# Two of four weight sums of each Strassen pair made by an accumulating DMA, with the weights stored as contiguous pairs of blocks

## Chip, cores and metric

One core of a Trainium2 chip runs the kernel. The metric is the device time of one execution in microseconds (us). TensorE is PE in the profile, VectorE is DVE, ScalarE is ACT, GpSimd is POOL and SyncE is SP.

## What is computed

A decoder block in float32 on 512 tokens of width 1024: two mixers side by side (retention with 4 heads, sliding-window attention with 8 query and 2 key heads), gated, merged and projected, then an MLP with squared ReLU of inner width 4096. Cut to what matters:

```python
h = rmsnorm(x, pre_mix_norm)
proj = h @ w_in                       # 1024 x 5888
q_r, k_r, v_r, g_r, q_s, k_s, v_s, gate_r, gate_s = split(proj)
y_r = (silu(g_r) * groupnorm(retention(q_r, k_r, v_r))) @ w_ret_out
y_s = sliding_window_attention(q_s, k_s, v_s, sinks) @ w_swa_out
merged = sigmoid(gate_r) * y_r + sigmoid(gate_s) * y_s
x = x + rmsnorm(merged @ w_out, post_mix_norm)
h = rmsnorm(x, pre_mlp_norm)
u = square(relu(h @ w_up))            # 1024 x 4096
x = x + rmsnorm(u @ w_down, post_mlp_norm)
```

The two gates are the last 2048 columns of `w_in`.

## The kernel before

Every product is made from split operands: `split` writes a float32 value as `hi + lo` (ACT casts `hi`, L106; DVE subtracts to get `lo`, L107), and `mm3` (L149 to L151) adds hi x hi, hi x lo and lo x hi in PSUM. A weight is loaded into a `raw` tile by SP (two buffers for the whole kernel) and split into `whi` and `wlo` (four buffers each).

The stages follow one another on PE: pre-norm and the first projections, four heads of retention and window attention, the window attention's output projection (`ys`), the gates with the retention's output projection (`yr`) between them, the output projection (`ps`), and the MLP.

For the gates and for 13 of the 16 pairs of `w_up` blocks, a pair of output blocks (256 columns) is made by one level of Strassen-Winograd: 7 block products instead of 8, each of 4 x 3 matmuls with 256 tokens. With the pair's weight cut into four quarters (`a11`, `a21` the first half of the contraction, `a12`, `a22` the second; the first index is the block of columns), `wino_weights` makes four sums:

- `s1 = a21 + a22` (L182) and `s3 = a11 + a21` (L183), the two halves of the tile `s31`, split into `p31`
- `s2 = s1 + a11` (L186) and `s4 = s2 + a12` (L187), the two halves of `s24`, split into `p24`

Besides, `p1` (`a11`, `a12`) and `p22` (`a22`) are splits of the quarters themselves. `p31` and `p1` lie in the `whi`/`wlo` buffers; `s31`, `s24`, `p24` and `p22` have one buffer each. `wino_pair` makes the products 11, s2, s1, s3, 12, s4 and 22 and combines them (DVE L218 to L229, ACT L217). `wino_tokens` makes the sums of the tokens once for the gates (`hsum`) and once for the MLP (`h2s`). Before the gates the tokens are put together as float32 in four places (`fb`): half of a `raw` buffer each for two, and the tiles `s31` and `s24` for the other two.

In the MLP the first three pairs of `w_up` blocks are plain products (`first_ups`, `up_half`, from `load_feature_pair`, L122), since half of the tokens come later. Then a quarter of a down projection (`load_moving`, L136, 48 matmuls of 512 columns) and an `up_pair` alternate; the last group has down projections alone.

The order on each engine is made by a scheduler when the kernel is built: by the order of the program, priorities (`tc.high_priority`) and its own estimate of when operands are ready. On the chip each engine keeps that order, and waits where an operand isn't there.

Of the kernel before, what the change touches and what calls it, by code (L numbers as in the profile page):

```python
# [20 lines left out]
KD = D_MODEL // P  # L21
# [7 lines left out]
EPS = 1e-6  # L29
# [8 lines left out]
C_QR, C_KR, C_VR, C_GR, C_QS, C_KS, C_GATE_R, C_GATE_S = (  # L38
    0, 512, 1024, 2048, 3072, 3584, 3840, 4864,
)  # L40
# [6 lines left out]
def decay_table():  # L47
    """[j, h, i]: gamma_h ** -(j + 1) / sqrt(dk) where i >= j, else 0; within a chunk."""
    pos = np.arange(P)
    t = np.where(  # L50
        pos[None, :] >= pos[:, None],
        np.exp(-log_gammas()[:, None, None] * (pos[:, None] + 1)), 0.0,
    )
    return np.ascontiguousarray((t * RET_DK**-0.5).transpose(1, 0, 2).astype(np.float32))


def chunk_table():
    """[j, 0, h]: gamma_h ** (127 - j) / sqrt(dk); [i, 1, h]: EPS * gamma_h ** (-2 (i + 1))."""
    pos, lg = np.arange(P)[:, None], log_gammas()[None, :]
    t = np.stack([np.exp(lg * (P - 1 - pos)) * RET_DK**-0.5, EPS * np.exp(-2 * lg * (pos + 1))], 1)  # L60
    return np.ascontiguousarray(t.astype(np.float32))


def distance_table():
    """[i, j]: distance of query i to key j of the two blocks, or MASKED / slope-free mask."""
    dist = (np.arange(P)[:, None] + P) - np.arange(2 * P)[None, :]
    return np.where((dist >= 0) & (dist < P), -dist, MASKED).astype(np.float32)

# [6 lines left out]
def block_kernel(ctx, tc, x, pre_mix, w_in, w_ret, w_swa, w_out, sinks, post_mix,  # L75
# [3 lines left out]
    w_in, w_ret, w_swa, w_out, w_up, w_down = (  # L79
        w[0] for w in (w_in, w_ret, w_swa, w_out, w_up, w_down)  # L80
    )
# [14 lines left out]
    def rstd_of(sumsq, n, scale):  # L96
        """(sumsq * scale + eps) ** -0.5, [P, n]."""
        ms = small.tile([P, 4], F32, name="ms")
        r = small.tile([P, 4], F32, name="rstd")
        nc.vector.tensor_scalar(ms[:, :n], sumsq, scale, EPS, op0=ALU.mult, op1=ALU.add)  # L100
        nc.gpsimd.tensor_tensor(r[:, :n], ms[:, :n], mhalf[:, :n], op=ALU.pow)
        return r

    def split(hi, lo, src):
        """src = hi + lo exactly, each with a significand that one pass carries."""
        nc.scalar.copy(hi, src)  # L106
        nc.vector.tensor_tensor(lo, src, f(hi), op=ALU.subtract)  # L107
# [10 lines left out]
    def load_feature_pair(w, c0):  # L118
        """Columns c0..c0+256 of w as two stationary blocks [k, kk, 128]."""
        nk = w.shape[0] // P  # L120
        raw = raw_tile([P, nk, 256])
        nc.sync.dma_start(raw, w[:, c0 : c0 + 256].rearrange("(k p) c -> p k c", p=P))  # L122
        return [parts(raw[:, :, b * P : (b + 1) * P], [P, nk, P]) for b in range(2)]

    def load_feature_blocks(w, cols):
        """Columns c..c+128 of w, for each c, as stationary blocks [k, kk, 128]."""
# [6 lines left out]
    def load_moving(w, r0, nr, c0, width):  # L133
        """Rows r0.. of w, columns c0..c0+width, as moving blocks, two tiles."""
# [24 lines left out]
    def wino_tokens(wx, b11, b12, b21, b22, f, dst):  # L159
        """b: (hi, lo) quadrants; f: their float32 copies, overwritten; dst: (hi, lo) of sums."""  # L160
# [13 lines left out]
    def wino_weights(wx, w, c0):  # L174
        """Columns c0..c0+256 of w: the seven left operands, (hi, lo) of [k, 4, 128]."""
        raw = raw_tile([P, KD, 256])
        nc.sync.dma_start(raw, w[:, c0 : c0 + 256].rearrange("(k p) c -> p k c", p=P))
        a11, a12 = raw[:, :4, :P], raw[:, 4:, :P]
        a21, a22 = raw[:, :4, P:], raw[:, 4:, P:]
        s31 = wx.tile([P, 2, 4, P], F32, name="s31")  # L180
        s24 = wx.tile([P, 2, 4, P], F32, name="s24")
        nc.vector.tensor_tensor(s31[:, 1], a21, a22, op=ALU.add)  # L182
        nc.vector.tensor_tensor(s31[:, 0], a11, a21, op=ALU.add)  # L183
        p31 = parts(s31, [P, 2, 4, P])
        p1 = parts(raw[:, :, :P], [P, KD, P])
        nc.vector.tensor_tensor(s24[:, 0], s31[:, 1], a11, op=ALU.add)  # L186
# [6 lines left out]
            "11": tuple(a[:, :4] for a in p1), "12": tuple(a[:, 4:] for a in p1),  # L193
            "22": tuple(p22),
            "s1": tuple(a[:, 1] for a in p31), "s3": tuple(a[:, 0] for a in p31),
# [3 lines left out]
    def wino_pair(wx, a, b, out):  # L199
        """out [P, 4, 256]: the two halves of block one, then those of block two, negated."""  # L200
# [30 lines left out]
    # ---- pools by phase  # L231
# [4 lines left out]
    def transpose_in(dst, src_of, half):  # L236
        """token-major [P, 1024] blocks (of two token blocks) -> feature-major hi, lo."""
# [13 lines left out]
    # ---- pre-norm of x, kv and first v projection by token block  # L251
# [22 lines left out]
    def norm_tokens(t):  # L274
        """Token block t of the normed input, transposed, as hi and lo."""
# [109 lines left out]
    def swa_scores(b, qs2):  # L385
        bias = dpool.tile([P, 2, 2 * P], F32, name="bias", bufs=2)
# [86 lines left out]
    # ---- retention, one head, by chunks of 128 tokens; token i of a chunk is carried  # L473
    # divided by gamma ** (i + 1), which the group norm takes out again
    def ret_keys(kT, h):
        """Token-major keys of the first three chunks, decayed to the chunk's end."""
# [24 lines left out]
    def ret_states(kd, v, h):  # L501
        """State before chunks 1, 2 and 3."""
# [114 lines left out]
    # ---- swa output projection  # L617
# [30 lines left out]
    # ---- gates  # L648
# [9 lines left out]
    fb = [fs[:, 0], fs[:, 1], wx.tile([P, 4, 256], F32, name="s31"), wx.tile([P, 4, 256], F32, name="s24")]  # L658
# [6 lines left out]
    def gate(name, bp):  # L665
        c0 = C_GATE_S if name == "s" else C_GATE_R
        a = wino_weights(wx, w_in, c0 + bp * 256)
# [14 lines left out]
    def ret_proj(bp):  # L682
        """Output projection of the retention, gated, plus the gated swa's, in sig."""
# [20 lines left out]
    # ---- output projections of both mixers, merge  # L704
# [33 lines left out]
    # ---- output projection, residual, pre-norm of the MLP  # L738
# [51 lines left out]
    # ---- MLP  # L790
# [19 lines left out]
    def up_half(fb, w, half):  # L810
        ps = bank([P, 256], "up")
        for k in range(KD):
            mm3(
                ps, (w[0][:, k, :], w[1][:, k, :]),
                tuple(a[:, k % 4] for a in quads[k // 4][half]), k == 0, k == KD - 1,
            )
        c = slice(half * 256, half * 256 + 256)
        rl = ppool.tile([P, 256], F32, name="rl")
# [20 lines left out]

    def first_ups(half, fps):  # L840
        for fp in fps:
            if half == 0 or fp == 0 and NH > 4:
                held[fp] = load_feature_pair(w_up, fp * 256)
# [23 lines left out]
    def up_pair(fp):  # L867
        a = wino_weights(wx, w_up, fp * 256)
# [16 lines left out]
    def finish(t, n):  # L885
        """Post-norm and residual of token block t, once acc's column half n is whole."""
# [72 lines left out]
_INS = ['x', 'pre_mix_norm', 'w_in', 'w_ret_out', 'w_swa_out', 'w_out', 'sinks', 'post_mix_norm',  # L959
# [20 lines left out]
```

## Time and profile before

| | |
|---|---|
| median of three runs | 774.61 us (774.47 to 774.65) |
| span of the profiled execution, first to last instruction | 772.8 us |
| the profiled execution's own time | no figure beside its span; the runs' median is 1.8 us above the span |
| PE busy | 761.1 us (98%), 4772 matmuls |
| DVE / ACT / POOL busy | 510.3 / 367.6 / 19.2 us |
| DMA | 78.21 MB, 101 GB/s in the mean |
| mean granted clock of TensorE | 0.997 |

Stages by the first matmul of each: gates from 254.0 us, output projection from 378.4, first up pairs from 423.7, Strassen up pairs and down projections from 460.2. A row of the timeline gives start and duration in us, engine (SPq is SP's queue of DMA issues), line, operation, output and inputs, shape, and in brackets how long the engine had been idle and what released it. A row of the waits gives who waited for what, then us in total, times, and the longest.

### The profile page before, as it was taken

The page shows a single profiled execution, that of the slowest core. Times are in us where ns is not written, and L with a number is a line of the kernel's source. Part 1 is how long each engine was busy: PE and PEld are TensorE (multiplying, and loading weights), DVE is VectorE, ACT ScalarE, POOL GpSimd, SP SyncE. Part 2 cuts the span into 40 slices and gives each one's busy share as a digit, 9 for nine tenths or more (in the row PEclk, how much of TensorE's full clock was granted, in tenths as well). Part 3 has the DMA queues.
Part 4 walks back from the last instruction along what each step waited for, and adds up shares of the span by engine and source line. Part 5 has one row for each costly group of instructions (what it writes and reads, how often), then busy time and mean ns, then how long its engine had stood idle before and what let it go on. Part 6 is the DMA issues. An engine that isn't in the chain of part 4 may idle for free.

```text
span 772.8 us, 11585 instructions
## 1 busy us (share of the span) xinstructions
PE 761.1 (98%) x4772; PEld 686.5 (89%) x4772; DVE 510.3 (66%) x841; ACT 367.6 (48%) x619; POOL 19.2 (2%) x30
## 2 busy tenths in 40 slices
PE   8999999999999999999999999999999999999996
PEld 6989889898888999999888999999999999999885
DVE  5474474655878888775954887665667675766364
ACT  6364454364644535333634785545544444444321
POOL 1100000000001000000011000000000000000000
PEclk9999999999999999999999999999999999999998
DMA  9151222312012333243571133333323333222402
GB/s 295 28 163 53 90 58 75 109 29 81 28 58 80 120 125 115 68 146 109 185 251 54 56 109 109 110 109 110 93 81 100 109 110 109 87 81 106 137 1 109
DMA packets 68038, 78.21 MB, mean 101 GB/s; under 512 B 1809, under 2 KB 55185, under 8 KB 67986
## 3 DMA queue, kind: packets, MB, share of 16 engines
q1 hardware_dynamic: 67986, 77.48, 31.3%
q8 instruction: 37, 0.61, 0.3%
q14 instruction: 15, 0.12, 0.1%
HBM read 75.38 MB, written 2.10 MB: 100 GB/s over the span
## 4 chain that ended last, share of the span: by engine, by line
PE 93%; DVE 3%; ACT 1%; issue 1%; DMA 1%; POOL 0%; SPq 0%; DVEq 0%; POOLq 0%; ACTq 0%
PE wino L149 9%; PE wino L151 9%; PE wino L150 9%; PE down L149 7%; PE down L150 7%; PE down L151 7%; PE pblk L151 5%; PE pblk L150 5%; PE pblk L149 5%; PE ptok L151 2%; PE ptok L150 2%; PE ptok L149 2%; PE yr L149 2%; PE ps L149 2%; PE ps L151 2%; PE yr L151 2%
## 5 line engine op out<-in xcount | busy, mean ns | idle before, releaser
L106 ACT CAST whi<-raw 128x1024 fp32r<-128x1024 f32 x103 | 107.9, 1051 | 127.1 <-PE down L151 57.7
L107 DVE TENSOR_TENSOR wlo<-raw,whi 128x1024 fp32r<-128x1024 f32 x103 | 125.4, 1221 | 63.0 <-ACT whi L106 53.6
L149 PE MATMUL down<-whi,u 128*128 128x512 f32 x256 | 99.8, 390 | 0.0
L150 PE MATMUL down<-wlo,u 128*128 128x512 f32 x256 | 99.7, 390 | 0.0
L151 PE MATMUL down<-whi,u 128*128 128x512 f32 x256 | 99.6, 389 | 0.0
L151 PE MATMUL pblk<-hT,wlo 128*128 128x512 f32 x160 | 62.4, 390 | 0.5 <-DVE wlo L107 0.5
L149 PE MATMUL pblk<-hT,whi 128*128 128x512 f32 x160 | 62.6, 391 | 0.0
L150 PE MATMUL pblk<-hT,whi 128*128 128x512 f32 x160 | 62.3, 390 | 0.0
L151 PEld LDWEIGHTS down<-whi,u 128*128 128x128 f32 x256 | 48.1, 188 | 10.0
L149 PEld LDWEIGHTS down<-whi,u 128*128 128x128 f32 x256 | 48.1, 188 | 9.6
L150 PEld LDWEIGHTS down<-wlo,u 128*128 128x128 f32 x256 | 48.1, 188 | 9.6
L149 PE MATMUL ptok<-whi,hT 128*128 128x256 f32 x160 | 46.1, 288 | 0.3 <-ACT hT L106 0.3
L106 ACT CAST whi<-s 128x1024 fp32r<-128x1024 f32 x21 | 22.0, 1049 | 51.1 <-PE wino L150 26.3
L151 PE MATMUL ptok<-whi,hT 128*128 128x256 f32 x160 | 45.4, 283 | 0.8 <-DVE hT L107 0.8
L150 PE MATMUL ptok<-wlo,hT 128*128 128x256 f32 x160 | 45.4, 284 | 0.0
L107 DVE TENSOR_TENSOR u<-rl,u 128x512 fp32r<-128x512 f32 (+1 forms) x38 | 22.1, 605 | 24.5 <-ACT u L106 24.5
L221 DVE TENSOR_TENSOR q<-wino,q 128x512 f32<-128x512 f32 x21 | 14.5, 691 | 34.4 <-PE wino L151 34.4
L151 PEld LDWEIGHTS pblk<-hT,wlo 128*128 128x128 f32 x160 | 30.0, 188 | 7.2 <-DVE wlo L107 0.9
L149 PEld LDWEIGHTS pblk<-hT,whi 128*128 128x128 f32 x160 | 30.1, 188 | 5.8
L150 PEld LDWEIGHTS pblk<-hT,whi 128*128 128x128 f32 x160 | 30.0, 188 | 5.8
L151 PEld LDWEIGHTS ptok<-whi,hT 128*128 128x128 f32 x160 | 30.6, 192 | 1.1 <-DVE hT L107 1.1
L149 PEld LDWEIGHTS ptok<-whi,hT 128*128 128x128 f32 x160 | 30.8, 192 | 0.7 <-ACT hT L106 0.7
(261 smaller groups left out, 2118.6 us busy)
## 6 DMA issues: line engine op xcount, KB each, us to landing
raw<-in_w_in SPq DMA_DIRECT2D x17, 1024.0 KB, 5.2
raw<-in_w_up SPq DMA_DIRECT2D x17, 1024.0 KB, 5.6
raw<-in_w_down SPq DMA_DIRECT2D x16, 1024.0 KB, 4.9
raw<-in_w_in SPq DMA_DIRECT2D x12, 512.0 KB, 4.4
raw<-in_w_ret_out SPq DMA_DIRECT2D x4, 1024.0 KB, 5.2
raw<-in_w_out SPq DMA_DIRECT2D x4, 1024.0 KB, 5.0
xt<-in_x SPq DMA_DIRECT2D x4, 512.0 KB, 8.1
raw<-in_w_swa_out SPq DMA_DIRECT2D x4, 512.0 KB, 3.5
```

What stands on the lines that cost most here:

```text
L106: nc.scalar.copy(hi, src)
L107: nc.vector.tensor_tensor(lo, src, f(hi), op=ALU.subtract)
L149: nc.tensor.matmul(ps, ah, bh, start=first, stop=False)
L150: nc.tensor.matmul(ps, ah, bl, start=False, stop=False)
L151: nc.tensor.matmul(ps, al, bh, start=False, stop=last)
L221: nc.vector.tensor_tensor(q[:, 1:3], p57, q[:, 0:1].to_broadcast([P, 2, 256]), op=ALU.add)
```

## The change

On the host, `pair_blocks` lays the gates' columns and `w_up` out by pair: for each pair and each of the 128 partitions, the four quarters one after the other, in the order `a22, a21, a11, a12`, 2 KB each. `w_in` keeps its first 3840 columns.

`wino_load` fills a `raw` tile of five quarters (10 KB in each partition, before 8 KB): SP loads `a21, a11` into places 3 and 4, `a11, a12` into places 0 and 1, and `a22` into place 2. POOL then issues a DMA that reads `a22, a21` from memory and adds them to places 3 and 4, which so become `s1` and `s3`. `wino_weights` keeps the other two sums on DVE and splits `p1` ahead of `p31`; the tile `s31` is gone, and `fb` uses `p240` in its place.

The plain up pairs load their four quarters in one DMA; in their second block the contraction's halves are in the other order, which `kw` follows. Also, `bias` of the window attention has one buffer instead of two, `rl` of the plain up pairs goes into the two-buffer tile `pc`, and the scratch for POOL's DMA descriptors is 1024 instead of 64.

```diff
+def pair_blocks(w):
+    nk, npair = w.shape[0] // P, w.shape[1] // 256
+    t = w.reshape(2, nk // 2, P, npair, 2, P).transpose(3, 2, 4, 0, 1, 5)
+    return np.ascontiguousarray(
+        np.stack([t[:, :, 1, 1], t[:, :, 1, 0], t[:, :, 0, 0], t[:, :, 0, 1]], 2)
+    )
...
-    def wino_weights(wx, w, c0):
-        raw = raw_tile([P, KD, 256])
-        nc.sync.dma_start(raw, w[:, c0 : c0 + 256].rearrange("(k p) c -> p k c", p=P))
-        a11, a12 = raw[:, :4, :P], raw[:, 4:, :P]
-        a21, a22 = raw[:, :4, P:], raw[:, 4:, P:]
-        s31 = wx.tile([P, 2, 4, P], F32, name="s31")
+    def wino_load(w):
+        raw = raw_tile([P, 5, 4, P])
+        nc.sync.dma_start(raw[:, 3:5], w[:, 1:3])
+        nc.sync.dma_start(raw[:, 0:2], w[:, 2:4])
+        nc.sync.dma_start(raw[:, 2], w[:, 0])
+        nc.gpsimd.dma_start(raw[:, 3:5], w[:, 0:2], accum_op=ALU.add)
+        return raw
+
+    def wino_weights(wx, raw):
+        s31 = raw[:, 3:5]
+        a11, a12, a22 = raw[:, 0], raw[:, 1], raw[:, 2]
         s24 = wx.tile([P, 2, 4, P], F32, name="s24")
-        nc.vector.tensor_tensor(s31[:, 1], a21, a22, op=ALU.add)
-        nc.vector.tensor_tensor(s31[:, 0], a11, a21, op=ALU.add)
+        p1 = parts(raw[:, :2], [P, 2, 4, P])
         p31 = parts(s31, [P, 2, 4, P])
-        p1 = parts(raw[:, :, :P], [P, KD, P])
-        nc.vector.tensor_tensor(s24[:, 0], s31[:, 1], a11, op=ALU.add)
+        nc.vector.tensor_tensor(s24[:, 0], s31[:, 0], a11, op=ALU.add)
         nc.vector.tensor_tensor(s24[:, 1], s24[:, 0], a12, op=ALU.add)
...
-        bias = dpool.tile([P, 2, 2 * P], F32, name="bias", bufs=2)
+        bias = dpool.tile([P, 2, 2 * P], F32, name="bias", bufs=1)
...
-    fb = [fs[:, 0], fs[:, 1], wx.tile([P, 4, 256], F32, name="s31"), wx.tile([P, 4, 256], F32, name="s24")]
+    fb = [fs[:, 0], fs[:, 1], wx.tile([P, 4, 256], F32, name="p240"), wx.tile([P, 4, 256], F32, name="s24")]
...
-        a = wino_weights(wx, w_in, c0 + bp * 256)
+        a = wino_weights(wx, wino_load(w_gate[i]))
...
+            kw = (k + 4) % KD if fb % 2 else k
             mm3(
-                ps, (w[0][:, k, :], w[1][:, k, :]),
+                ps, (w[0][:, kw, :], w[1][:, kw, :]),
...
-        rl = ppool.tile([P, 256], F32, name="rl")
+        rl = wx.tile([P, 256], F32, name="pc", bufs=2)
...
+    def load_up_pair(fp):
+        raw = raw_tile([P, 4, 4, P])
+        nc.sync.dma_start(raw, w_up[fp])
+        return [
+            parts(raw[:, q : q + 2].rearrange("p q k c -> p (q k) c"), [P, KD, P]) for q in (2, 0)
+        ]
...
-                held[fp] = load_feature_pair(w_up, fp * 256)
+                held[fp] = load_up_pair(fp)
...
-        a = wino_weights(wx, w_up, fp * 256)
+        a = wino_weights(wx, wino_load(w_up[fp]))
```

More of the change, by code (lines that the diff above doesn't have):

```diff
@@ L36 @@
 QS_AT = 1
-C_QR, C_KR, C_VR, C_GR, C_QS, C_KS, C_GATE_R, C_GATE_S = (
-    0, 512, 1024, 2048, 3072, 3584, 3840, 4864,
-)
+C_QR, C_KR, C_VR, C_GR, C_QS, C_KS, C_GATE_R = (0, 512, 1024, 2048, 3072, 3584, 3840)
 def log_gammas():
@@ L74, in block_kernel @@
 @with_exitstack
-def block_kernel(ctx, tc, x, pre_mix, w_in, w_ret, w_swa, w_out, sinks, post_mix,
+def block_kernel(ctx, tc, x, pre_mix, w_in, w_gate, w_ret, w_swa, w_out, sinks, post_mix,
                  pre_mlp, w_up, w_down, post_mlp, decay, chunk, dist, out):
@@ L78, in block_kernel @@
     x, out = x[0], out[0]
-    w_in, w_ret, w_swa, w_out, w_up, w_down = (
-        w[0] for w in (w_in, w_ret, w_swa, w_out, w_up, w_down)
-    )
+    w_in, w_ret, w_swa, w_out, w_down = (w[0] for w in (w_in, w_ret, w_swa, w_out, w_down))
     const = ctx.enter_context(tc.tile_pool(name="const", bufs=1))
@@ L192, in wino_weights @@
         return {
-            "11": tuple(a[:, :4] for a in p1), "12": tuple(a[:, 4:] for a in p1),
+            "11": tuple(a[:, 0] for a in p1), "12": tuple(a[:, 1] for a in p1),
             "22": tuple(p22),
-            "s1": tuple(a[:, 1] for a in p31), "s3": tuple(a[:, 0] for a in p31),
+            "s1": tuple(a[:, 0] for a in p31), "s3": tuple(a[:, 1] for a in p31),
             "s2": tuple(a[:, 0] for a in p24), "s4": tuple(a[:, 1] for a in p24),
@@ L665, in gate @@
     def gate(name, bp):
-        c0 = C_GATE_S if name == "s" else C_GATE_R
-        a = wino_weights(wx, w_in, c0 + bp * 256)
+        i = bp + (KD // 2 if name == "s" else 0)
+        a = wino_weights(wx, wino_load(w_gate[i]))
         if name == "s":
@@ L956, in block_kernel @@
                     up_pair(nxt + 2 * n + q)
-_INS = ['x', 'pre_mix_norm', 'w_in', 'w_ret_out', 'w_swa_out', 'w_out', 'sinks', 'post_mix_norm',
+_INS = ['x', 'pre_mix_norm', 'w_in', 'w_gate', 'w_ret_out', 'w_swa_out', 'w_out', 'sinks', 'post_mix_norm',
         'pre_mlp_norm', 'w_up', 'w_down', 'post_mlp_norm']
@@ L965 @@
     from concourse.bass_utils import run_bass_kernel_spmd
-    nc = bacc.Bacc("TRN2", target_bir_lowering=False, num_devices=1, dynamic_dma_scratch_size=64)
+    nc = bacc.Bacc("TRN2", target_bir_lowering=False, num_devices=1, dynamic_dma_scratch_size=1024)
     arrays, args = {}, []
+    w_in = np.asarray(inputs["w_in"])
+    inputs = dict(
+        inputs, w_in=w_in[:, :, :C_GATE_R], w_gate=pair_blocks(w_in[0, :, C_GATE_R:]),
+        w_up=pair_blocks(np.asarray(inputs["w_up"])[0]),
+    )
     given = [(n, np.ascontiguousarray(inputs[n])) for n in _INS]
```

## The prediction

> **What bounds the kernel now.** I read the page's busy table first, then the chain that ended last, then the waits of PE alone, because only a wait of PE can be shortened here.
>
> ```profile
> PE 761.1 (98%) x4772; PEld 686.5 (89%) x4772; DVE 510.3 (66%) x841; ACT 367.6 (48%) x619; POOL 19.2 (2%) x30
> PE 93%; DVE 3%; ACT 1%; issue 1%; DMA 1%; POOL 0%; SPq 0%; DVEq 0%; POOLq 0%; ACTq 0%
> ```
>
> PE is busy for 761.1 of the 772.8 us span, and 93% of the chain runs on it. DVE, from which the change takes work, stands at 66%. So what counts is how often PE waits:
>
> ```profile
> PE g_pre L270 <- DMA g_row<-in_pre_mix_norm: 2.3, 1, 2.3
> PE ptok L151 <- DVE hT L107: 0.8, 1, 0.8
> PE wino L149 <- ACT whi L106: 0.5, 1, 0.5
> PE pblk L151 <- DVE wlo L107: 0.5, 1, 0.5
> ```
>
> Only the third is beside a Strassen weight, and it happens once: the first gate. By stage, the table of busy time in stretches says the same:
>
> ```profile
> 254.00:378.00 124.00, 123.98 (x863) 116.49 (x864) 98.94 (x139) 54.94 (x73) 0.00 (x0) 1.00 0.34 111
> 460.00:723.00 263.00, 263.00 (x1676) 240.12 (x1675) 172.24 (x232) 124.54 (x177) 0.00 (x0) 1.00 0.33 106
> ```
>
> The columns are stretch and length, then PE, PEld, DVE, ACT and POOL busy, the granted clock, the DMA share and GB/s. In the gates (254 to 378) and in the MLP's Strassen part (460 to 723) PE has no idle time at all, at the full clock. DVE work taken away there is worth nothing by itself; POOL is wholly idle there.
>
> **The change part by part.** *Sums removed from DVE.* Two of the four sums of each pair go:
>
> ```profile
> L182 DVE TENSOR_TENSOR s<-raw 128x512 f32<-128x512 f32 x21 | 14.5, 690 | 23.6 <-DMA raw<-in_w_up 21.1 <-DMA raw<-in_w_in 2.2
> ...
> L183 DVE TENSOR_TENSOR s<-raw 128x512 f32<-128x512 f32 x21 | 14.4, 685 | 0.0
> ```
>
> 21 x 0.69 + 21 x 0.685 = 28.9 us of DVE, from 510.3 to about 481. On the path: nothing, except at the first gate.
>
> *The first gate.* Now `s31` is a tile that also holds a token copy (`fb[2]`), so the first pair's sums wait until the token sums are done:
>
> ```profile
> 250.64 0.69 DVE L182 TENSOR_TENSOR s<-raw 128x512 f32<-128x512 f32 x1
> ...
> 252.90 0.39 PE L150 MATMUL ys<-swaT,whi 128*128 128x512 f32 x1
> 253.13 0.39 PE L151 MATMUL ys<-swaT,wlo 128*128 128x512 f32 x1
> 254.01 0.39 PE L149 MATMUL wino<-hT,whi 128*128 128x256 f32 x1 [0.50 <-ACT whi L106]
> ```
>
> Starts are in the first column, durations in the second; matmuls overlap. The last two `ys` matmuls start 0.23 apart, so the next could start at 253.13 + 0.23 = 253.36; it starts at 254.01, 0.65 late. After the change `s31` lies in `raw`, and `p1` (which the product "11" needs) comes first in program order and waits for one load alone. The products 11, s1, s3 and 12 then need nothing that is made after 250.64 except token sums. Gain 0.65 us. Ends: 0 if the wait passes to another operand, 0.65.
>
> *Loads.* One load of 1024 KB becomes three on SP (512, 512, 256 KB) and one accumulating load of 512 KB on POOL: 1.75 times the bytes, in longer contiguous pieces.
>
> ```profile
> raw<-in_w_in SPq DMA_DIRECT2D x17, 1024.0 KB, 5.2
> raw<-in_w_up SPq DMA_DIRECT2D x17, 1024.0 KB, 5.6
> raw<-in_w_down SPq DMA_DIRECT2D x16, 1024.0 KB, 4.9
> raw<-in_w_in SPq DMA_DIRECT2D x12, 512.0 KB, 4.4
> xt<-in_x SPq DMA_DIRECT2D x4, 512.0 KB, 8.1
> raw<-in_w_swa_out SPq DMA_DIRECT2D x4, 512.0 KB, 3.5
> ```
>
> (Last column: median us from issue to landing.) No row shows an accumulation. Its lower end is 3.5 us, a plain 512 KB; its upper end in rows is 8.1 us, 512 KB in the crowded start. I take 5.4 us, between the two 1024 KB rows 5.2 and 5.6, since 512 KB from HBM and 512 KB of the destination have to be read. Ahead of it stands the first 512 KB load, 4.4 us, and POOL's wake-up and issue, for which I take 1.0 us (SP's issue rows below show 0.37, the POOL row below 1.98). So the sums arrive 10.8 us after SP's issue; the ends are 3.5 + 0.4 + 3.5 = 7.4 and 8.1 + 2.0 + 8.1 = 18.2, the upper one only if both loads meet a crowd like the start's. Bandwidth is there: 0.79 MB more in each of 12 pairs within 263 us add 36 GB/s to 106, at a DMA share of 0.33 so far.
>
> *Where that lateness meets a deadline: the MLP's steady stretch.* One cycle (a quarter of a down projection and an up pair, 21 us):
>
> ```profile
> 493.48 0.37 SPq L177 DMA_DIRECT2D raw<-in_w_up  x1
> 499.06 0.69 DVE L182 TENSOR_TENSOR s<-raw 128x512 f32<-128x512 f32 x1 [1.68 <-DMA raw<-in_w_up]
> 500.27 0.69 DVE L186 TENSOR_TENSOR s<-s,raw 128x512 f32<-128x512 f32 x1
> 502.14 1.23 DVE L107 TENSOR_TENSOR wlo<-raw,whi 128x1024 fp32r<-128x1024 f32 x1 [0.46 <-ACT whi L106]
> 508.05 1.05 ACT L106 CAST whi<-s 128x1024 fp32r<-128x1024 f32 x1 [2.39 <-PE wino L150]
> 512.52 0.40 PE L150 MATMUL down<-wlo,u 128*128 128x512 f32 x1
> ```
>
> The sums themselves aren't needed before ACT's cast at 508.05, which waits for PE to give back a `whi` buffer. They would be there at 493.48 + 10.8 = 504.3. But DVE takes its queue in order: if the remaining sums (L186, L187, 2 x 0.69) keep their place, they hold the down weights' `wlo` (502.14) behind them, which PE wants at 512.52. The landing may be as late as 512.52 - 1.23 - 1.38 = 509.9: 5.6 us to spare. Cost 0; if the cover is gone, every us beyond comes once per cycle, 12 times. The release of `raw` stays where it is, since its last reader is still the split of `p22`, which waits for PE.
>
> *The tightest place: the second gate pair,* whose load goes out only when the token sums leave their `raw` buffer:
>
> ```profile
> 248.25 0.37 SPq L177 DMA_DIRECT2D raw<-in_w_in  x1
> 262.89 1.05 ACT L106 CAST p<-s 128x1024 fp32r<-128x1024 f32 x1
> 264.20 0.28 PE L149 MATMUL wino<-hT,whi 128*128 128x256 f32 x1
> 264.40 0.69 DVE L229 TENSOR_TENSOR sgr<-wino,q 128x512 f32<-128x512 f32 x1 [0.20 <-PE wino L151]
> 265.64 0.28 PE L149 MATMUL wino<-hsum,p 128*128 128x256 f32 x1
> ```
>
> PE starts this pair at 264.20 and asks for `p24` at 265.64. Two sums (1.38) and the cast (1.05) stand between, so the landing may come at 263.2; it is expected at 248.25 + 10.8 = 259.05, 4.1 us earlier. Accumulations over 9.5 us would stall PE here, once. Cost 0, upper end 18.2 - 14.9 = 3.3 us.
>
> *POOL's queue.* POOL waits for the first load before it can issue, and what is queued behind it waits too. From 254 on that is only the `pow` of later norms, long after the last gate; ahead of it lies one close neighbour:
>
> ```profile
> 233.16 1.98 POOL L546 TENSOR_TENSOR rr<-rms,mhalf 128x4 f32<-128x4 f32 x1 [32.40 <-DVE rms L545]
> 235.18 1.90 DVE L548 TENSOR_SCALAR retn<-ret_v,mv,rr 128x256 f32<-128x256 f32 x4 [0.90 <-POOL rr L546]
> 238.87 0.38 PE L558 MATMUL ret_t<-ident,retn 128*128 128x128 f32 x2
> 230.50 0.37 SPq L177 DMA_DIRECT2D raw<-in_w_in  x1
> ```
>
> The first gate's load is issued at 230.50 and lands its first half at 234.9, after the `pow` became ready; I assume the `pow` stays first. Cost 0.
>
> *The rest.* SP issues two more loads per pair, 2 x 0.37 us; SP waits for buffers anyway.
>
> ```profile
> 1.55 5.95 DMA raw<-in_w_in
> ...
> 384.95 21.65 SPq L122 DMA_DIRECT2D raw<-in_w_up  x4
> ...
> 423.68 0.28 PE L149 MATMUL up<-h2c,whi 128*128 128x256 f32 x1
> ...
> L394 DVE TENSOR_SCALAR bias<-dist_sb x8: 270/290/294, 31.1 to 104.7; 128x256 f32<-128x256 f32 x8
> ```
>
> The first three up pairs become contiguous loads, split as before; all four of their issues are over at 406.6, 17 us ahead of PE's first use at 423.68: 0, and with that cover gone at most the 0.7 us between the 4.9 and 5.6 rows. `w_in` has shorter rows: its first load, the one in the chain that ended last, could change as those rows differ from 5.2, by -0.3 to +0.4; I take 0. `bias` gets one buffer: DVE writes the last of them at 104.7, a whole head ahead, and may now write it once the head before has been read; 0, or 2 x 0.29 per head without that cover. `rl` of the first up pairs gets two buffers for one: 0, since ACT alone waits there.
>
> **Sum.** 772.8 - 0.65 = 772.15 us of span. The runs' median is 774.61, 1.81 above this span; that part I keep. 772.15 + 1.81 = 773.96: **774.0 us**, 0.08% faster, which no measurement of this kernel can tell from no change (that takes about 0.2%, 1.55 us).
>
> **The rivals.** *A, slower: accumulations over 11 us.* A per-element add in the transfer may be far slower than a copy; nothing in the trace says no. At 12 us the second gate is 2.5 us late and each of 12 cycles 1.0 us: 774.0 + 14.5 = 788 us. It decides from 11.0 us on. For it: no row bounds an accumulation. Against: rows of twice its bytes take 5.6 us, and only PE's wish for `wlo`, not the sums, sets the limit. 0.12.
>
> *B, slower: POOL's issue is held up by a busy DVE.* At the second gate DVE is without a gap from 250.64 to 264.40, where 0.20 us idle stand. If POOL got its accumulation out only then, the sums would land at 264.4 + 5.4 = 269.8, 6.6 us late: 780.6 us. In the MLP the 1.68 us gap before 499.06 covers the issue. Against it: nothing in the trace shows POOL held by DVE. 0.08. [...]
>
> *C, slower: the order on POOL.* If the first gate's accumulation stands ahead of the `pow` at 233.16, that `pow` starts at 234.9 + 1.0, 2.7 us late, and with it `retn`, the transposes at 238.87 and the token sums: 776.7 us at most. Against: the `pow` is older in program order and ready first. 0.08.
>
> *D, faster.* The narrower `w_in` rows shorten the first weight load, on which the start hangs, by up to 1.05 (from 5.95 in the chain to the 4.9 of `w_down`), and the 0.65 comes on top: 774.6 - 1.7 = 772.9 us. 0.07.
>
> *E, the forecast,* with the case that the 0.65 doesn't come (774.6): 0.65.
>
> **Numbers.** Faster 0.07 (D), same 0.65 (E), slower 0.28 (A, B, C). The range takes in D and C and leaves out A and B, 0.20: 772.8 to 777.5 us. The forecast's own range is 773.4 to 775.5.
>
> **What would show it.** Right: DVE busy near 481 us; no PE wait at the first gate; POOL DMAs that land within 9.5 us of their issue; 263 us still without PE idle between 460 and 723. Wrong: PE waits on `whi`, `wlo` or `p24` in each up pair, with DVE idle before the sums on the accumulating transfer (A); PE waiting about 6 us once at the second gate (B); a late `rr` (C); a first `ptok` matmul over half a us earlier (D).

## The result, and the profile after

The changed kernel takes 782.58 us in the median of four runs (781.39 to 783.58), the kernel before 774.63 beside it: a ratio of 1.0093, interval 1.0078 to 1.0107 (the two medians alone give 1.0103). 774.0 was forecast, and the upper end of the range was 777.5. The profiled execution has a span of 780.5 us against 772.8, and a time of its own of 782.28.

One thing is needed to read the ratios below: the kernel before comes out near 774.6 or near 775.9 us, which I put down to its first matmuls (the first term below), and the profile of the prediction has the lower value. Each ratio is against the runs of the kernel before that stand beside it, whose median was 775.77 to 776.06 in the experiments. That start apart, the change costs 6.4 us in the two traces, as the table below shows.

The page of the changed kernel, busy time and the chain that ended last:

```profile
PE 765.6 (98%) x4772; PEld 689.9 (88%) x4772; DVE 481.2 (62%) x799; ACT 367.8 (47%) x619; POOL 37.9 (5%) x51
PE 95%; DVE 2%; issue 1%; DMA 1%; ACT 0%; SPq 0%; DVEq 0%; POOLq 0%; POOL 0%; ACTq 0%
```

DVE lost the 29 us, and PE, with the same 4772 matmuls, is busy for 4.5 us more. So part of the loss lies inside "busy": matmuls that run slower or further apart. The waits of PE show the other part:

```profile
PE wino L157 <- DVE p L113: 3.1, 1, 3.1
...
PE wino L155 <- ACT p L112: 0.5, 1, 0.5
```

Each happened once. The same stages in the table of busy time in stretches (gates, then MLP), and below them the place of the wait, cut finer:

```profile
254.00:385.00 131.00, 127.34 (x865) 118.46 (x864) 88.47 (x123) 54.94 (x73) 6.18 (x7) 0.99 0.52 149
467.00:730.00 263.00, 263.00 (x1679) 240.24 (x1678) 152.52 (x207) 122.25 (x172) 10.45 (x12) 1.00 0.50 140
267.00:270.70 3.70, 0.50 (x2) 0.30 (x2) 3.70 (x5) 0.54 (x2) 0.00 (x0) 1.00 0.05 13
270.70:274.20 3.50, 3.49 (x18) 3.49 (x19) 1.57 (x3) 1.53 (x3) 0.72 (x1) 0.58 0.96 282
274.20:277.00 2.80, 2.80 (x24) 2.80 (x23) 0.44 (x1) 0.51 (x1) 0.15 (x1) 0.92 1.05 373
```

The MLP stands as before: 263.00 of 263 us. The gates are where PE idles. After the idle stretch comes one with a granted clock of 0.58 (the value ahead of the DMA share). A clock of 1 for t us and of one half for the rest gives 0.58 x 3.5 = 2.03 = t + (3.5 - t)/2, so t = 0.56; in the next row 0.92 x 2.8 leaves 0.45 us of half clock. So the half clock ran from 271.26 to 274.65, 3.4 us (the column reads 0.50 for just this stretch), and cost half of that, 1.7 us.

To see what each stage added, I compared the starts of the same matmuls in both traces (the last column is taken from unrounded starts):

| first matmul of | before | after | added by the stage ahead |
|---|---|---|---|
| first `pblk` | 34.48 | 35.80 | +1.32 |
| first gate pair | 254.01 | 254.87 | -0.46 |
| second gate pair | 264.20 | 264.95 | -0.11 |
| first `yr` | 274.30 | 280.68 | **+5.64** |
| output projection (`ps`) | 378.38 | 385.96 | **+1.19** |
| first up pair | 423.68 | 431.30 | +0.04 |
| end of the span | 772.79 | 780.51 | +0.11 |

Three terms, each in one place. The first is the start:

```profile
12.00:15.50 3.50, 3.50 (x32) 3.31 (x30) 2.83 (x6) 3.50 (x6) 0.56 (x1) 1.00 1.10 345
```

is before, and in the same 3.5 us of the changed kernel stand 19 matmuls where there were 32:

```profile
12.00:15.50 3.50, 3.50 (x19) 3.50 (x19) 2.83 (x6) 2.85 (x4) 0.56 (x1) 1.00 1.08 345
```

They start 0.21 us apart instead of 0.12, about twice as far, though the clock column says 1.00 here. The experiments show this term with and without the accumulation: between 13.00 and 15.50 us stand 15 matmuls in the changed kernel and 15 in its variant with the sums made by DVE, but 23 in the kernel before and 24 in the variant with the accumulation in the MLP alone. And of two variants of the kernel before with the same `yr` matmuls, the first `yr` starts at 274.5 us in one (256 bytes in front) and at 276.0 in the other (512 bytes at the other end). So I take it for the start's two values, and not for the change.

The second term, 5.64 us, is the second gate pair. Its timeline:

```profile
249.90 0.33 SPq L184 DMA_DIRECT2D raw<-in_w_gate  x1
254.70 0.88 POOL L187 DMA_DIRECT2D raw<-in_w_gate  x1 [16.90 <-DMA raw<-in_w_gate]
262.68 0.69 DVE L197 TENSOR_TENSOR s<-raw 128x512 f32<-128x512 f32 x1 [4.80 <-DMA raw<-in_w_gate]
265.17 0.69 DVE L198 TENSOR_TENSOR s<-s,raw 128x512 f32<-128x512 f32 x1
268.30 1.22 DVE L113 TENSOR_TENSOR wlo<-raw,whi 128x1024 fp32r<-128x1024 f32 x1
269.43 1.22 DVE L113 TENSOR_TENSOR p<-s,p 128x1024 fp32r<-128x1024 f32 x1
267.07 0.39 PE L155 MATMUL wino<-hsum,p 128*128 128x256 f32 x1 [0.52 <-ACT p L112]
267.29 0.28 PE L156 MATMUL wino<-hsum,p 128*128 128x256 f32 x1
270.71 0.39 PE L157 MATMUL wino<-hsum,p 128*128 128x256 f32 x1 [3.13 <-DVE p L113]
```

SP's first load landed after 4.8 us, POOL issued at once, and the accumulated sums were there at 262.6, 12.7 us after SP's issue. DVE had stood idle for 4.80 us, with all its later work queued behind the blocked sum. From 262.68 on it caught up, and only at 269.43 came `lo` of `p24` (the row `p<-s,p`), which PE had wanted just after 267.29. The hi part came from ACT (0.52 late), the lo part 3.13 late. Had only its own chain stood between (two sums, the cast and the subtraction, 1.38 + 1.05 + 1.22 us from 262.68), `lo` would have been there at 266.3, ahead of the time at which PE wanted it; so the delay is DVE's queue, read from these rows. No run moved `p24` forward in that queue. The rest of the 5.64, 1.99 us, is the half clock's 1.7 and 0.3 that isn't traced.

The third term is in the four pairs of `yr` blocks, 0.29 us each. Two groups of instructions by tile (min, median and max in ns, first and last start), with two rows of the timeline:

```profile
L155 PE MATMUL yr<-retT,whi x64: 397/398/400, 280.7 to 385.3; 128*128 128x512 f32 x64
...
312.28 0.40 PE L156 MATMUL yr<-retT,whi 128*128 128x512 f32 x1
312.51 0.40 PE L157 MATMUL yr<-retT,wlo 128*128 128x512 f32 x1
```

and the same group before:

```profile
L149 PE MATMUL yr<-retT,whi x64: 389/389/396, 274.3 to 377.7; 128*128 128x512 f32 x64
```

The matmuls start 233 ns apart in the mean instead of 227: 192 x 6 ns = 1.2 us. Nothing waits there.

### The profile page after: what moved, and what is told of

It reads as the page before. It is cut to its first block, busy times and chain, and to the rows that moved or that the text cites. A ratio compares the mean times of both kernels' runs of the same rounds, so it can differ in the third digit from the quotient of the medians.

```text
span 780.5 us, 11735 instructions
## 1 busy us (share of the span) xinstructions
PE 765.6 (98%) x4772; PEld 689.9 (88%) x4772; DVE 481.2 (62%) x799; ACT 367.8 (47%) x619; POOL 37.9 (5%) x51
## 4 chain that ended last, share of the span: by engine, by line
PE 95%; DVE 2%; issue 1%; DMA 1%; ACT 0%; SPq 0%; DVEq 0%; POOLq 0%; POOL 0%; ACTq 0%
PE wino L157 9%; PE wino L155 9%; PE wino L156 9%; PE down L155 7%; PE down L156 7%; PE down L157 7%; PE pblk L157 5%; PE pblk L155 5%; PE pblk L156 5%; PE ptok L157 2%; PE ptok L155 2%; PE ptok L156 2%; PE yr L157 2%; PE yr L155 2%; PE yr L156 2%; PE ps L157 2%
## 5 line engine op out<-in xcount | busy, mean ns | idle before, releaser
L112 ACT CAST whi<-raw 128x1024 fp32r<-128x1024 f32 x124 | 130.2, 1054 | 169.1 <-PE wino L156 52.2
L113 DVE TENSOR_TENSOR wlo<-raw,whi 128x1024 fp32r<-128x1024 f32 x124 | 150.0, 1219 | 59.1 <-ACT whi L112 51.4
L197 DVE TENSOR_TENSOR s<-raw 128x512 f32<-128x512 f32 x21 | 14.5, 692 | 97.6 <-DMA raw<-in_w_up 74.9
L895 ACT ACTIVATE rl<-rl 128x512 f32<-128x512 f32 x26 | 15.0, 626 | 44.9 <-DVE rl L240 44.9
L113 DVE TENSOR_TENSOR u<-rl,u 128x512 fp32r<-128x512 f32 x26 | 17.0, 689 | 27.4 <-ACT u L112 27.4
L157 PEld LDWEIGHTS ptok<-whi,hT 128*128 128x128 f32 x160 | 31.4, 196 | 1.1 <-DVE hT L113 1.1
L155 PEld LDWEIGHTS ptok<-whi,hT 128*128 128x128 f32 x160 | 31.6, 197 | 0.7 <-ACT hT L112 0.7
```

Source lines behind the costliest of these rows:

```text
L155: nc.tensor.matmul(ps, ah, bh, start=first, stop=False)
L157: nc.tensor.matmul(ps, al, bh, start=False, stop=last)
L197: nc.vector.tensor_tensor(s24[:, 0], s31[:, 0], a11, op=ALU.add)
L895: nc.scalar.activation(r, r, AF.Relu, scale=(1.0, -1.0)[b])
```

## The experiments

The two candidates for the 5.64 us were, first, that the accumulation as such is too slow everywhere and the gate is only the first to show it, and second, the place: only this pair's load is held until the token sums leave its `raw` buffer. For `yr`, traffic of the transfers stood against where tiles lie in memory. "After" and "before" name the kernel an edit starts from.

**The second pair's load set free.** The token copies go into `sgr` buffers, which are idle then, so both `raw` buffers are free early.

```diff
-    fs = raw_tile([P, 2, 4, 256])
-    fb = [fs[:, 0], fs[:, 1], wx.tile(...
+    fs = [sgpool.tile([P, 4, 256], F32, name="sgr", bufs=4) for _ in range(2)]
+    fb = [fs[0], fs[1], wx.tile(...
```

> The changed kernel with one edit: the two token copies that lay in a raw buffer lie in two tiles of sgpool instead, so that the second gate pair's loads need not wait for the token sums. Theory Q (the late landing of the second pair's accumulated sums blocks DVE and ACT in order, and PE waits for the p24 that stands at the end of DVE's backlog): the second pair's loads leave some 15 us earlier, the 3.3 and 0.7 us waits of PE at 267 to 271 vanish, and with them the half clock of 3.4 us after them (1.7 us): 782.6 - 5.6 = about 777 us. Rival S (the new static order around p24 with its one buffer makes the wait, whenever the sums land): the waits stay, about 782 us.

Measured: 778.36 us (777.44 to 779.83), ratio 1.0032 (1.0019 to 1.0045). POOL's timeline and PE's waits of this kernel:

```profile
236.40 0.91 POOL L187 DMA_DIRECT2D raw<-in_w_gate  x1 [1.04 <-DMA raw<-in_w_gate]
```

```profile
PE wino L155 <- ACT p L112: 0.3, 1, 0.3
PE wino L157 <- DVE p L113: 0.3, 1, 0.3
```

The accumulation goes out 18 us earlier, and the 3.1 us wait and the half clock in mid-run are gone: the granted clock is 1.00 from 254 to 385, where the changed kernel has 0.99. A part of the gain was lost elsewhere: by the starts, the first gate pair takes 0.66 us more than in the changed kernel, and the gates from the first `yr` on 1.13 more. The two waits for `p24` above, one in the first pair and one in a later gate, are 0.6 of that; the rest isn't traced.

**All but one pair as in the change.** The sharper form: only the second gate pair is loaded plainly, and DVE makes its sums.

```diff
+    def wino_load_dve(w):
+        raw = raw_tile([P, 5, 4, P])
+        nc.sync.dma_start(raw[:, 2:4], w[:, 0:2])
+        nc.sync.dma_start(raw[:, 0:2], w[:, 2:4])
+        nc.vector.tensor_tensor(raw[:, 4], raw[:, 3], raw[:, 2], op=ALU.add)
+        nc.vector.tensor_tensor(raw[:, 3], raw[:, 0], raw[:, 3], op=ALU.add)
+        return raw
...
+        if name == "s" and bp == 0:
+            a = wino_weights(wx, wino_load_dve(w_gate[i]), 1)
```

> The changed kernel with the accumulation undone for one pair of 21, the second gate pair (two plain loads, both sums by DVE); all else as changed, the token copies in raw too. Theory Q: this one pair carries the waits and the halved clock: 782.6 - 4.0 - 1.7 = about 777 us, no PE wait over 1.5 us after the start. Rival: if other pairs' accumulations or the late load of this pair alone make the waits, about 780 us or more.

Measured: 777.00 (775.42 to 778.06, ten runs), ratio 1.0017 (1.0007 to 1.0027). Its gates in the table of stretches:

```profile
254.00:378.00 124.00, 124.00 (x858) 115.71 (x858) 88.29 (x123) 53.71 (x72) 5.29 (x6) 1.00 0.51 148
```

PE has no idle time left, with 20 of 21 accumulations in place. The stage ahead of the first `yr` adds -0.01 us here (+5.64 in the changed kernel): one pair carried the whole term. What is left of the ratio, 0.17% or 1.3 us, is the size of the `yr` term (1.19 us in its trace, too).

**The sums by DVE, the new layout kept.** One 1024 KB load per pair, one instruction for both sums, and the `raw` tile and the scratch as large as before.

```diff
-        raw = raw_tile([P, 5, 4, P])
-        nc.sync.dma_start(raw[:, 3:5], w[:, 1:3])
...
-        nc.gpsimd.dma_start(raw[:, 3:5], w[:, 0:2], accum_op=ALU.add)
+        raw = raw_tile([P, 4, 4, P])
+        nc.sync.dma_start(raw, w)
...
+        s31 = wx.tile([P, 2, 4, P], F32, name="s31")
+        nc.vector.tensor_tensor(s31, raw[:, 0:2], raw[:, 1:3], op=ALU.add)
```

> The changed kernel without the accumulating DMA: the same contiguous layout, one load of 1024 KB per pair into a tile of four quarters, and s1 and s3 made by DVE in one instruction; descriptor scratch 64 as before. Theory Q: no PE wait over 1 us at the second gate, yr at 227 ns (operands at 96 and 96 again), time within 1.5 us of the kernel before (773.9 to 776), the spread being the clock of the start. Rival S: the waits at the second gate stay, about 780 us. Rival L (the new layout's loads or the narrower w_in rows cost the time): about 780 us, in the start or in the loads.

Measured: 775.81 (774.52 to 776.82), ratio 1.0003 (0.9992 to 1.0013). So the layout in pairs of blocks and the smaller edits are worth nothing either way. This profile also shows the start's half clock in its own column:

```profile
13.00:15.50 2.50, 2.50 (x15) 2.50 (x13) 2.36 (x3) 2.11 (x4) 0.10 (x1) 0.54 1.11 330
```

**The accumulation in the MLP alone,** with the tiles moved back in step (next experiment).

```diff
-        a = wino_weights(wx, wino_load(w_gate[i]))
+        a = wino_weights(wx, wino_load_dve(w_gate[i]), 1)
```

> The changed kernel with the accumulating DMA in the MLP alone: the eight gate pairs are loaded by two plain loads and DVE makes s1 and s3, s3 in the place of a21; a constant tile of 64 bytes in front, which takes out the slower yr. Theory Q: the 13 accumulations of the MLP cost PE nothing, though DVE waits 75 us for them in all; no PE wait over 1 us anywhere after the start; the time of the kernel before, 774.5 to 776 as its start goes. If the accumulations of the MLP carry a part of the loss by traffic or order: over 777 us.

Measured: 775.81 (774.76 to 776.51), ratio 1.0004 (0.9994 to 1.0013).

```profile
460.00:723.00 263.00, 263.00 (x1677) 240.15 (x1676) 153.18 (x206) 122.19 (x171) 10.57 (x12) 1.00 0.50 140
```

Thirteen accumulations take 19 us of work from DVE in this stretch (172.24 before), and the time stays: as forecast, no gain and no loss.

**64 bytes at the front of memory.** The change shifts the left-hand tiles by 5056 bytes per partition (960 of descriptor scratch, 2 x 2048 of `raw`), so `whi` starts at 22176 instead of 17120, while `retT`, allocated from the other end, stays at 180192. A tile of 64 bytes ahead of all others makes the shift 5120.

```diff
+    const.tile([P, 16], F32, name="pad64")
```

> The changed kernel with a constant tile of 64 bytes per partition in front, which moves everything on the left side of SBUF by 64 bytes and nothing on the right side (retT, swaT). Theory A (a matmul of 512 columns is slower when the addresses of its two operands stand at different places within 128 bytes, as whi at 32 and retT at 96 do now, against 96 and 96 before): the start-to-start distance of the yr matmuls falls from 233 back to 227 ns and of ys from 229 to 227: 192 x 6 ns + 96 x 2 ns = 1.3 us less, about 781.3 us. Rival T (the accumulating transfers' traffic in the gates slows the reads of PE): yr stays at 233 ns, no change in the time.

Measured: 781.40 (780.71 to 782.56), ratio 1.0074 (1.0055 to 1.0093).

```profile
L156 PE MATMUL yr<-retT,whi x64: 389/389/396, 281.7 to 385.6; 128*128 128x512 f32 x64
```

`yr` runs as before, and the second gate's waits stay. In these matmuls that is 1.2 us less, by a tile that nothing reads. The times alone don't show it: their ranges overlap, and in this profile the second gate's waits were 4.4 us where the changed kernel had 3.65.

**The same 64 bytes in the kernel before,** then 128 (`[P, 32]`), then 256 (`[P, 64]`), and 512 at the other end, which moves `retT`.

```diff
+    const.tile([P, 16], F32, name="pad64")
```

> The kernel before with a constant tile of 64 bytes per partition in front, nothing else. Theory A: yr rises from 227 to 233 ns and ys to about 229, all other matmuls stay: 774.6 + 1.3 = 775.9 us. Rival T: yr stays at 227 ns, 774.6 us. On the start (theory C: when the full clock is granted in the first 16 us is chance from run to run; the PE work there is the same): the clock may come near 10.6 or near 15.3 us in the profile, independent of the kernel.

> The kernel before with 128 bytes in front instead of 64. Theory A (only the place within 128 bytes counts): yr back at 227 ns, time of the kernel before. If any shift of the left side against the right side costs, yr is 233 ns again as with 64 bytes.

> The kernel before with 256 bytes in front. 64 and 128 bytes made yr slow (233 and 232 ns), 5120 bytes did not (227). Theory A2 (the distance between the two operands counts by its remainder in 256): yr 227 ns. Theory A3 (by its remainder in 512 or 1024): yr 232 or 233 ns.

> The kernel before with a tile of 512 bytes behind retT and swaT, which moves these two by 512 bytes and the left side not at all. If the remainder in 256 or in 512 counts: yr 227 ns. If the remainder in 1024 counts: yr 232 or 233 ns.

Measured: 777.02 (775.61 to 778.53), ratio 1.0014 (1.0004 to 1.0024) with 64 bytes; 776.78 (775.61 to 778.06), 1.0014 (1.0005 to 1.0023) with 128; one run each of 774.78 with 256 and 776.25 with 512 at the other end, which is too few to tell a quarter of a per cent, so the group of matmuls decides. In that order, with 64, 128, 256 and 512 at the other end:

```profile
L150 PE MATMUL yr<-retT,whi x64: 394/394/403, 275.5 to 380.1; 128*128 128x512 f32 x64
```

```profile
L150 PE MATMUL yr<-retT,whi x64: 390/393/404, 274.4 to 378.7; 128*128 128x512 f32 x64
```

```profile
L150 PE MATMUL yr<-retT,whi x64: 389/389/396, 274.5 to 377.9; 128*128 128x512 f32 x64
```

```profile
L149 PE MATMUL yr<-retT,whi x64: 389/389/396, 276.0 to 379.4; 128*128 128x512 f32 x64
```

With 64 and with 128 bytes `yr` starts every 232.5 to 233.5 ns, with 256, 512 and 5120 every 227. The kernel before has no accumulating transfer, so their traffic isn't the cause. The 1.2 us come from where the operands lie: shifts that are multiples of 256 bytes were harmless, and 64, 128 and 5056 (192 over a multiple) were not. A theory by which 128 bytes would be harmless already falls. Matmuls with both operands on the left, as `pblk` and `down`, didn't change (a median of 389 ns in the kernel before, in the changed one and with 128 bytes), though their operands moved by the same bytes; from that I take it that the place of one operand against the other counts, and not a place alone. No run moved `retT` by anything but a multiple of 256.

**The sums made later.** SP's loads change places, so the load that the accumulation waits for comes last.

```diff
-        nc.sync.dma_start(raw[:, 3:5], w[:, 1:3])
         nc.sync.dma_start(raw[:, 0:2], w[:, 2:4])
         nc.sync.dma_start(raw[:, 2], w[:, 0])
+        nc.sync.dma_start(raw[:, 3:5], w[:, 1:3])
```

> The changed kernel with the three plain loads of a pair in another order: the half that the accumulation needs goes last instead of first, behind 768 KB. A dose of lateness: from the rows of the changed kernel (512 KB 5.3 us, 1024 KB 5.4 us to landing) the accumulation is issued 1 to 2.5 us later. Theory Q: PE's waits at the second gate grow from 4.0 us by the same 1 to 2.5 us, 783.5 to 785 us; in the MLP's stretch, where by the trace DVE waits up to 7.9 us for the sums and PE never waits, there are still 5.6 - 1.8 us to spare, so nothing is added there. Rival S (the order around p24, not the landing): no change, about 782 us.

Measured: 791.21 (786.01 to 793.44), ratio 1.0194 (1.0152 to 1.0235), more than expected, because in the profiled execution the MLP, too, had a wait. Its timeline there, and the second gate's and the MLP's rows of the table of stretches:

```profile
600.15 0.87 POOL L187 DMA_DIRECT2D raw<-in_w_up  x1 [20.82 <-DVE acc L953]
609.59 0.69 DVE L197 TENSOR_TENSOR s<-raw 128x512 f32<-128x512 f32 x1 [9.09 <-DMA raw<-in_w_up]
617.24 0.33 SPq L184 DMA_DIRECT2D raw<-in_w_up  x1
629.78 0.69 DVE L197 TENSOR_TENSOR s<-raw 128x512 f32<-128x512 f32 x1 [7.65 <-DMA raw<-in_w_up]
630.39 1.22 DVE L113 TENSOR_TENSOR wlo<-raw,whi 128x1024 fp32r<-128x1024 f32 x1
631.67 0.80 PE L156 MATMUL down<-wlo,u 128*128 128x512 f32 x1 [3.57 <-DVE wlo L113]
```

```profile
269.00:275.90 6.90, 4.56 (x21) 4.57 (x22) 3.90 (x6) 1.52 (x3) 0.00 (x0) 0.51 0.66 202
630.80:637.70 6.90, 6.03 (x14) 4.78 (x15) 6.76 (x10) 1.65 (x3) 0.00 (x0) 0.51 0.49 152
```

That is the mechanism of rival A: the down weights' `wlo` behind a sum that isn't there. The accumulation of the cycle before, beside a load of `w_down` that went out 0.4 us after it, took 9.4 us from its issue to the sum, so that its buffer came back late, and the next pair's load went out at 617.24, 12.5 us ahead of its sum. In the MLP PE lost 3.57 us by the wait and about 3.4 more by 6.8 us of half clock; at the second gate it waited for 1.07 and 2.90 us (`p24`'s two parts again), with as long a half clock. There the forecast erred the other way: counted from SP's first issue, the accumulation went out 2.2 us later and the sums came 1.2 us later, but DVE, in another order, came to `p24`'s lo part 6.0 us behind the first sum instead of 6.75, so that PE's waits grew by 0.3 us where 1 to 2.5 were expected.

```profile
267.94 0.39 PE L155 MATMUL wino<-hsum,p 128*128 128x256 f32 x1 [1.07 <-ACT p L112]
271.34 0.58 PE L157 MATMUL wino<-hsum,p 128*128 128x256 f32 x1 [2.90 <-DVE p L113]
```

**A plain copy in place of the addition.** POOL's transfer overwrites instead of adding, so the sums are left out; the transfer, its wait and its place are the same.

```diff
-        nc.gpsimd.dma_start(raw[:, 3:5], w[:, 0:2], accum_op=ALU.add)
+        nc.gpsimd.dma_start(raw[:, 3:5], w[:, 0:2])
```

> The changed kernel with POOL's transfer as a plain copy of the same 512 KB to the same place: the addition is left out, so s1 and s3 are the quarters a22 and a21. It prices the addition itself. Theory D (an accumulation reads two operands and takes the time of twice its bytes): the copy lands in about 4.2 us after POOL's issue instead of 5.4 in the MLP and in about 6 instead of 7.7 in the gates, and PE's waits at the second gate shrink by the same 1.5 us, to about 2.5 us: 780 us. Rival W (the wait for the first load, POOL's issue and the crowd of loads make the lateness, not the addition): the copy lands as late as the accumulation, within 0.5 us, and the time stays near 782 us.

Measured: 779.73 (778.86 to 780.55), ratio 1.0055 (1.0036 to 1.0074). The table of DMA issues (last column: median us from issue to landing), of the changed kernel and of this one:

```profile
raw<-in_w_up POOLq DMA_DIRECT2D x13, 512.0 KB, 5.4
...
raw<-in_w_gate POOLq DMA_DIRECT2D x8, 512.0 KB, 7.7
```

```profile
raw<-in_w_up POOLq DMA_DIRECT2D x13, 512.0 KB, 4.5
raw<-in_w_gate POOLq DMA_DIRECT2D x8, 512.0 KB, 5.9
```

```profile
PE wino L157 <- DVE p L113: 2.6, 1, 2.6
```

The addition costs 0.9 us in the MLP and 1.8 in the gates, yet a copy in two steps would also be too late: the stage of the second gate adds 4.37 us with it, 5.64 with the addition. So the greater part is the chain of two transfers, and the addition the smaller.

**The start.** The first key and value block of the kernel before takes all of its products with the hi part of the tokens first, and those with the lo part, which DVE makes later, at the end.

```diff
+            for k in range(KD):
+                (ah, al), (bh, bl) = hcol(k, t), w_kv[k]
+                nc.tensor.matmul(ps, ah, bh, start=k == 0, stop=False)
+                nc.tensor.matmul(ps, ah, bl, start=False, stop=False)
+            for k in range(KD):
+                (ah, al), (bh, bl) = hcol(k, t), w_kv[k]
+                nc.tensor.matmul(ps, al, bh, start=False, stop=k == KD - 1)
```

> The kernel before with one edit at its start: for the first token block of kv the products with hi of the tokens are made for all k first, those with lo after them, so that PE doesn't wait 1.1 us for DVE's lo at 10.4 to 11.6 us. Theory C (the two levels of the kernel before, near 774.6 and 776.0 us, differ by whether the full clock is granted near 10.5 us or near 15 us, and a PE wait in the last window before decides it): the wait goes (1.0 us less) and the full clock comes near 10.5 us in nearly all runs: 773.0 to 774.0 us, with little spread. Rival: the two levels have another source; then the spread of 1.4 us stays and the time falls by 1.0 us at most, to 774.9 us in the median.

Measured: 774.62 (774.36 to 776.65, nine of ten runs under 774.9), ratio 0.9988 (0.9977 to 0.9999). The lower value didn't become lower: PE now waits 0.85 us for the hi part and 0.52 for the transposes' input, where it waited 0.33 for hi and 0.84 for lo. But the upper value became rarer. The same with the accumulation in the MLP:

> e7 (accumulation in the MLP alone, 64 bytes in front) with hi before lo for the first token block: the best version the runs point to. Theories Q, A and C: 774.3 to 774.6 us in nearly all runs, against two levels of 774.6 and 776.0 of the kernel before: 0.1% faster than its median. If the accumulations bring nothing at all, it equals e8 (774.6).

775.00 (774.45 to 776.77, twelve runs), ratio 0.9999 (0.9990 to 1.0008), and seven of the twelve at the lower value. So the reorder doesn't make the early clock sure; whether it helps at all is open, and that a wait of PE decides between the two values isn't shown.

**Towards the best version.** The token copies moved, the 64 bytes, and hi first, with all 21 accumulations:

> The changed kernel with all 21 accumulations kept and three repairs: the token copies in sgpool's tiles (as in e1), 64 bytes in front (as in e2), and hi before lo for the first token block (as in e8). By theories Q, A and C the sum is 778.36 - 1.2 (yr) - about 1.0 (start, most runs at the early clock) = about 776.1 us; what is left over the kernel before at its early clock (774.6) should be the waits of 0.3 to 0.5 us for p24 in the later gates. If it stays over 777.5, a cost is left that none of the theories names.

777.34 (776.81 to 778.18), ratio 1.0028 (1.0017 to 1.0038).

```profile
PE wino L158 <- DVE p L114: 1.3, 3, 0.6
PE wino L156 <- ACT p L113: 0.6, 1, 0.6
```

With the big wait gone, several small ones stand, up to 0.6 us, each for `p24`, and DVE works without a gap ahead of the one of 0.6 that is traced (no idle time from 286.53 to 298). Then one pair left to DVE, as above, with the 64 bytes and hi first:

> e12 (accumulation for all pairs but the second gate pair) with 64 bytes in front and hi before lo for the first token block. From e12's 777.0 us: yr 1.2 us less, and the start as in e8 in most runs. 774.3 to 775.8 us, with e12's profile 0.3 us ahead of the kernel before once yr is taken out: at best 0.2% faster than the kernel before in the median (775.8), no more.

774.78 (774.46 to 778.56, eleven runs) against 776.06, ratio 0.9988 (0.9978 to 0.9998). That is the ratio of hi first alone, 0.9988, and it is the start's: all 15 runs of the kernel before beside it had the upper value, and of the two traces, both with the lower one, the spans are 772.87 us here and 772.79 before. Twenty accumulations, placed where they hold up nothing, add nothing measurable to it.

## Why the prediction was wrong

*Sums removed from DVE, and their worth.* Right: 481.2 us of DVE where 481 were forecast, and no value in it, as the MLP alone shows.

*The first gate.* Nearly right: the stage ahead of it gave 0.46 us of the 0.65, and 0.66 in the kernel with the 64 bytes. The difference is `ys`, which reads `swaT` on the other side too: its matmuls start about 2 ns further apart (229.1 instead of 227.1 in the first 36, 230.5 instead of 228.3 in the other 60).

*Loads, and the MLP's steady stretch.* Right for this kernel: the accumulation took 5.4 us, the value chosen (whether for the reason given, twice the bytes to read, isn't shown), POOL's issue 0.88, where 1.0 was taken, and PE didn't idle. DVE shows the price that nobody paid:

```profile
DVE s L197 <- DMA raw<-in_w_up: 74.9, 12, 7.9
```

It waits 12 times, up to 7.9 us. The "5.6 us to spare" were too many, though: they took the landing as steady, and the run with late sums had one at 9.4 us that carried over into the next cycle.

*The tightest place: the second gate pair.* This step failed, and it put a cost of 0 where 5.64 us stood. It named the place and erred four times there. The landing came 12.7 us after SP's issue instead of 10.8, since the accumulations of the gates, beside the other loads there, took 7.7 us in the median instead of 5.4; that ate 1.9 of "4.1 us earlier". SP's issue came 1.65 us later and the pair itself only 0.75, which ate another 0.9; 1.3 us would still have been left. The deadline was wrong: "two sums (1.38) and the cast (1.05) stand between" counts what `p24`'s hi part needs. PE asks for the lo part as well, and that stands on DVE behind everything that queued up while the sum blocked: from 262.68 to 269.43, 6.75 us, where 1.38 were counted. The MLP paragraph above it had counted exactly that kind of work behind the sums; here it was left out. The trace before shows how little was left for lo:

```profile
265.01 1.22 DVE L107 TENSOR_TENSOR p<-s,p 128x1024 fp32r<-128x1024 f32 x1
266.36 0.30 PE L151 MATMUL wino<-hsum,p 128*128 128x256 f32 x1
```

It was ready at 266.23, and PE took it 0.13 us later. And the price of a wait was put at its own length. PE's waits of 3.65 us cost 5.64, and 1.7 of that is the clock that fell by half. The upper end named, 3.3 us, was therefore too low, too. The granted clock was a half for 3.4 us with the pause of 3.13 us here (0.50 from 271.26 to 274.65), for as long with the 2.6 us of the run with the copy (0.50 from 269.60 to 273.00, 1.00 behind it), and in the run with late sums for 6.8 us (0.51 over 6.90), both with the 1.07 and 2.90 us at the gate and with the 3.57 in the MLP. What sets these lengths isn't shown.

*POOL's queue.* Right; `pow` stays first:

```profile
234.47 1.98 POOL L557 TENSOR_TENSOR rr<-rms,mhalf 128x4 f32<-128x4 f32 x1 [32.40 <-DVE rms L556]
236.74 1.06 POOL L187 DMA_DIRECT2D raw<-in_w_gate  x1 [0.29 <-issue]
```

*The rest.* Loads of the first up pairs, `bias` and `rl`: 0.04 us, right. Missing from it was a term that no instruction has: the bigger `raw` tile and scratch moved the tiles on one side by 5056 bytes, and that cost 1.2 us in `yr`.

*The sum.* Forecast span 772.15, found 780.5: 5.64 (second gate) + 1.19 (`yr`) + 1.32 (the start, not the change's) + 0.2 (first gate, less than counted) make 8.35 of the 8.36 us.

*The rivals.* A, accumulations over 11 us, didn't happen in this kernel (5.4 and 7.7), but its mechanism is what the run with late sums shows. B, POOL held by a busy DVE, didn't happen: POOL issued at 254.70, as soon as the first load had landed, and the first sum followed 8 us later. DVE had a gap just then (253.95 to 255.12), so this place can't show whether a busy DVE would have held POOL. Another can: here DVE is busy through the whole issue (another TENSOR_TENSOR ends at 445.76), and it took 0.91 us, as against 0.88 in the gap. That is shown for TENSOR_TENSOR alone.

```profile
445.52 0.91 POOL L187 DMA_DIRECT2D raw<-in_w_up  x1 [6.56 <-DVE acc L168]
445.67 1.22 DVE L170 TENSOR_TENSOR acc<-acc 128x1024 f32<-128x1024 f32 x1
```

C and D didn't come, by the rows of `pow` and of the start. The true case was in none of them: a queue that fills up behind a wait.

## What to carry to other kernels

When a wait moves onto an engine that takes its queue in order, as DVE did here (in the run with late sums it stood idle for 7.65 us ahead of a sum, with `wlo` behind it), ask what else stands in that engine's queue: the deadline is the time at which PE needs the last of the work that piles up behind the wait, not that of the direct successors, and it has to be read at each place where the load is issued late. In a stream that PE bounds, price a wait at more than its own length: here 3.65 us of waits cost 5.64, with 3.4 us of half clock. When a tile changes its size, look at the spacing of matmuls whose operands lie on both sides of it; keep the shift a multiple of 256 bytes, as the harmless ones here were.

## What the runs showed of the hardware

- An accumulating transfer of 512 KB from memory into SBUF took 5.4 us in the MLP and 7.7 in the gates, a plain one from the same queue 4.5 and 5.9 (medians). POOL was busy for 0.9 us in the mean with an accumulating issue (0.874 in the MLP, 0.905 in the gates) and for 0.54 with two plain ones in the gates, 0.72 with the first.
- The `yr` matmuls of 512 columns, one operand on each side, started every 227 ns where one side was shifted by 0, 256, 512 or 5120 bytes, and every 232.5 to 233.5 where it was shifted by 64, 128 or 5056. Why isn't shown.
- With a longest pause of PE of 2.6 to 3.6 us the granted clock was a half for 3.4 us in two kernels (3.13 us in the changed one, 2.6 with the copy) and for 6.8 in two places of a third, the one with late sums (2.90 and 3.57 us). What decides between the two isn't settled. Shorter waits in mid-run brought none: the clock is 1.00 over the gates of the kernel before, with one of 0.50 us, and of the variant with the token copies moved, with two of 0.3.
- At the start the matmuls stood 0.12 us apart from 11.84 us on in the trace of the kernel before, and 0.21 apart until 15.2 us in the changed one's, where the first `pblk` came 1.32 us later. In two variants of the changed kernel 24 and 15 of them started between 13.00 and 15.50 us, with the accumulation in the MLP alone and without any.
